# Left factors asked for sooner, and eighteen idle matmuls between the first transposes, in a two-layer decoder trunk

## The chip, the cores and the metric

One core of a Trainium2 chip (trn2) runs the kernel. The metric is the device time of one execution in microseconds (us); the time given is the median of several plain runs. A profiled execution is one run more, taken with the hardware profiler.

## The reference

The input is x of 512 positions by 1024 features, in float32. Two layers follow one another, each a mixer and a feed-forward, each with an RMS norm ahead and a residual add behind.

```python
for i in range(DEPTH):                       # DEPTH = 2
    hn = rmsnorm(h, mix_norm_g[i])
    if i % 2 == 0:
        h = h + sgu_mixer(hn, ...)           # gelu(hn @ w_in) -> u, v; LN(v) mixed over 128 positions; (u * mixed) @ w_out
    else:
        h = h + retention(hn, positions, ...)  # q, k rotated, decayed scores, v, gated by silu(g); @ w_out
    h = h + swiglu(rmsnorm(h, ffn_norm_g[i]), ...)   # (silu(a) * b) @ w_down, a and b 2816 wide
return rmsnorm(h, final_norm_g)
```

## The kernel before, in words

**Matrix products.** Every float32 product is made of three matmuls (`three`, L246): each factor is split into a high part in the fast fp32r format (`h`) and the rest (`l`), and h·h, h·l and l·h are summed in PSUM. For the weights ScalarE (ACT) writes `wh_...` (L216) and VectorE (DVE) writes `wl_...` = raw - `wh` (L223).

**Seven products instead of eight.** The large products (`seven`, L321) split both factors in quarters and use a Strassen-like scheme with the seven products P1, P7, P6, Q4, P5, P2, P3. For each of them the weight tile is a quarter or a sum of quarters. Such a sum is made in part by a DMA that adds while it writes: the first quarter is loaded through SyncE's queue (SP, L344), the next is added by a DMA that GpSimd (POOL) issues (L347). P6's weights come into being in P7's tile: once DVE has written P7's `wl`, POOL's DMA adds one more quarter to the raw tile, and ACT makes P6's `wh` from it. The raw tile's name in the program keeps the label P722 for all of P7, P6 and Q4.

**Left factors.** The other side, the activations, has sums as well. `combos` (L473) makes them for products whose left side is computed in the kernel, `xA` (L709) for the normed x of a feed-forward or of the retention. Each sum is a `Chain` of three steps: `total` (DVE, `xP7_...`, L737), `high` (ACT, `xP7h_...`, L740) and `low` (DVE, `xP7l_...`, L743). Asking for a sum (`ask=True`) runs the first step; each later job of the pipeline runs one more; a use without `ask` runs what is left. Asking sooner therefore moves these steps forward in the recorded order.

**The order.** `pipeline` (L92) records the jobs; a scheduler in the framework then orders the instructions of each engine by a timing model of its own. Every engine works off its own queue strictly in that order. A small move in the source can thus reorder several queues.

**The start.** x comes in four chunks of 128 positions. PE first runs five idle matmuls on a tile of ones (`wake`, L174 to L177), then transposes chunk 0 (`xT_in_0`, eight 128x128 transposes, L669), `mix_ps` (a small transpose of the gains, L193), and chunk 1 (`xT_in_1`) as soon as its load is there. ACT and DVE make the halves `XH_in` and `XL_in` of each chunk (L673, L674). The first projection (`ps_v0`, in two PSUM tiles for chunks 0 and 1 and for chunks 2 and 3) works chunk by chunk with four weight tiles of 512 KB, `wr_v0_0` to `wr_v0_3`, whose halves `wh_v0_i`, `wl_v0_i` are scaled by `mix_cols` (L219, L226).

**The end of the first mixer.** `into_x("so", ...)` multiplies by `sgu_w_out` and adds to `X`. Its last product P3 (PSUM tile `X_so`, left factor `y_P3h`, `y_P3l`) is made for two chunks, 12 matmuls each. After each, DVE adds to `X` (L530), ACT squares (`sq_so`), small DVE instructions make the norm's factor (`nf_so`), DVE scales (`xs_f0_c`, L687), PE transposes (`xT_f0_c`), and ACT and DVE make `XH_f0` and `XL_f0` of chunk c. Chunks 3 and 2 are done before P3, chunks 0 and 1 behind it.

**The first feed-forward's opening.** `project_t("gl0", ...)` (PSUM `ps_gl0`, weights `wh_gl0_k`) first runs on chunks 2 and 3, then P1 of unit 0 (`X_gu0_0`, 48 matmuls), also on chunks 2 and 3; then the rest of `gl0` on chunks 0 and 1; then P7 (`Y_gu0_0`), which needs `xP7h_f0` and `xP7l_f0`. The second layer's feed-forward (`..._f1`, `gl1`, `gu1`) is built in the same way.

## Time and profile before

| | before |
|---|---|
| median of 3 plain runs | 1204.01 us (1203.71 to 1204.62) |
| the profiled execution | 1207.73 us |
| its span, first to last instruction | 1206.0 us |
| PE (TensorE) busy | 1186.8 us, 98% |
| DVE (VectorE) busy | 924.9 us, 77% |
| ACT (ScalarE) busy | 644.4 us, 53% |
| POOL (GpSimd) busy | 160.8 us, 13% |
| mean granted TensorE clock | 0.996 |

A row of a timeline gives the start and the length in us, the engine, the source line, the operation and its tiles (without buffer numbers), the shapes, the count of merged instructions, and in brackets the idle time ahead of it with what ended it. `[3.09 <-DMA X<-in_x]` reads: idle for 3.09 us until the load of X landed. The window rows give, for each engine, busy us and count, and at the end the mean granted clock of TensorE, the mean busy share of the DMA engines, and GB/s. The rows of the chain of waits have start, length and what ran. Matmuls overlap: the recorded length of one is more than the distance to the next.

### The profile page before, as it was taken

How to read it: one execution, taken by the hardware profiler on the slowest of the kernel's cores; microseconds unless marked ns; L12 is line 12 of the kernel's file. 1: busy time of each engine (PE TensorE's matmuls, PEld its weight loads, DVE VectorE, ACT ScalarE, POOL GpSimd, SP SyncE). 2: the span in 40 equal slices, each digit the busy share in tenths (PEclk: the TensorE clock that was granted, in tenths of full speed). 3: DMA queues.
4: the chain of work that ended last, by engine and by line, in shares of the span. 5: the costliest groups of instructions: out<-in, count | busy, mean ns of one | idle time of the engine just before them, and what ended most of it. 6: DMA issues, size and time to landing. Idle time of an engine off the chain costs nothing.

```text
span 1206.0 us, 18055 instructions
## 1 busy us (share of the span) xinstructions
PE 1186.8 (98%) x7206; PEld 1064.2 (88%) x7206; DVE 924.9 (77%) x1095; ACT 644.4 (53%) x815; POOL 160.8 (13%) x143
## 2 busy tenths in 40 slices
PE   8999999999999999999999999999999999999997
PEld 6888799998999987888888888888899989999986
DVE  5587968698987698788674757879768697666897
ACT  5523657455444547655453645566555554454565
POOL 1000121121110130211101001130121021101210
PEclk9999999999999999999999999999999999999999
DMA  9912958777876787766566457878867788676892
GB/s 312 282 48 57 243 118 204 184 165 213 210 196 153 198 170 255 192 140 176 113 190 143 119 133 171 204 131 283 215 125 174 191 222 203 165 195 187 156 245 96
DMA packets 118981, 216.42 MB, mean 179 GB/s; under 512 B 7497, under 2 KB 20849, under 8 KB 118897
## 3 DMA queue, kind: packets, MB, share of 16 engines
q1 hardware_dynamic: 83888, 148.13, 36.7%
q0 software_dynamic: 34720, 66.61, 33.1%
q8 instruction: 56, 0.92, 0.3%
q10 hardware_dynamic: 288, 0.52, 0.1%
q14 instruction: 29, 0.23, 0.1%
HBM read 212.10 MB, written 2.10 MB: 178 GB/s over the span
## 4 chain that ended last, share of the span: by engine, by line
PE 88%; DMA 4%; issue 3%; DVE 2%; ACT 2%; POOL 1%; SPq 0%; DVEq 0%; POOLq 0%; ACTq 0%
PE X_gu L249 6%; PE X_gu L248 6%; PE X_gu L247 6%; PE Y_gu L248 3%; PE Y_gu L249 3%; PE Y_gu L247 3%; PE X_dn L247 3%; PE X_dn L248 3%; PE X_dn L249 3%; PE X_vg L247 2%; PE X_vg L248 2%; PE X_vg L249 2%; PE ps_qk L247 2%; PE ps_qk L248 2%; PE ps_qk L249 2%
## 5 line engine op out<-in xcount | busy, mean ns | idle before, releaser
L223 DVE TENSOR_TENSOR wl_gu_P<-wr_gu_P,wh_gu_P 128x1024 fp32r<-128x1024 f32 x120 | 144.6, 1219 | 43.9 <-ACT wh_gu_P L216 43.8
L216 ACT ACTIVATE wh_gu_P<-wr_gu_P 128x1024 fp32r<-128x1024 f32 x120 | 122.4, 1051 | 64.4 <-DVE wr_gu_P L375 37.6
L347 POOL DMA_DIRECT2D wr_gu_P<-in_ffn_w_gu x48 | 58.4, 1244 | 384.8 <-DMA wr_gu_P<-in_ffn_w_gu 176.6
L216 ACT ACTIVATE wh_dn_P<-wr_dn_P 128x1024 fp32r<-128x1024 f32 x72 | 69.2, 980 | 50.2 <-DVE wr_dn_P L375 12.9
L223 DVE TENSOR_TENSOR wl_vg_P<-wr_vg_P,wh_vg_P 128x1024 fp32r<-128x1024 f32 x48 | 58.3, 1220 | 34.3 <-ACT wh_vg_P L216 28.0
L223 DVE TENSOR_TENSOR wl_dn_P<-wr_dn_P,wh_dn_P 128x1024 fp32r<-128x1024 f32 x72 | 79.4, 1128 | 2.5 <-issue 2.2
L347 POOL DMA_DIRECT2D wr_vg_P<-in_ret_w_in x26 | 31.5, 1250 | 262.9 <-DMA wr_vg_P<-in_ret_w_in 89.6
L347 POOL DMA_DIRECT2D wr_dn_P<-in_ffn_w_down x36 | 42.0, 1239 | 179.7 <-DMA wr_dn_P<-in_ffn_w_down 89.2
L216 ACT ACTIVATE wh_vg_P<-wr_vg_P 128x1024 fp32r<-128x1024 f32 x48 | 49.6, 1055 | 27.9 <-DMA wr_vg_P<-in_ret_w_in 13.0
L248 PE MATMUL ps_qk<-XL_r,wh_qk 128*128 128x512 f32 (+1 forms) x160 | 55.6, 348 | 0.0
L247 PE MATMUL ps_qk<-XH_r,wh_qk 128*128 128x512 f32 (+1 forms) x160 | 55.3, 348 | 0.0
L249 PE MATMUL ps_qk<-XH_r,wl_qk 128*128 128x512 f32 (+1 forms) x160 | 55.1, 348 | 0.0
L248 PE MATMUL Y_gu<-xP7l_f,wh_gu_P 128*128 128x256 f32 x160 | 45.4, 284 | 0.9 <-DVE xP7l_f L743 0.9
L247 PE MATMUL Y_gu<-xP7h_f,wh_gu_P 128*128 128x256 f32 x160 | 45.4, 284 | 0.8 <-ACT xP7h_f L740 0.8
L247 PE MATMUL Z_gu<-XH_f,wh_gu_P 128*128 128x256 f32 x160 | 45.4, 284 | 0.0
L249 PE MATMUL X_gu<-XH_f,wl_gu_P 128*128 128x256 f32 x160 | 45.3, 283 | 0.0
L247 PE MATMUL X_gu<-XH_f,wh_gu_P 128*128 128x256 f32 x160 | 45.3, 283 | 0.0
L248 PE MATMUL X_gu<-xP6l_f,wh_gu_P 128*128 128x256 f32 x160 | 45.3, 283 | 0.0
L249 PE MATMUL X_gu<-xP6h_f,wl_gu_P 128*128 128x256 f32 x160 | 45.3, 283 | 0.0
L247 PE MATMUL X_gu<-xP5h_f,wh_gu_P 128*128 128x256 f32 x160 | 45.3, 283 | 0.0
L248 PE MATMUL X_gu<-xP5l_f,wh_gu_P 128*128 128x256 f32 x160 | 45.3, 283 | 0.0
L249 PE MATMUL X_gu<-xP5h_f,wl_gu_P 128*128 128x256 f32 x160 | 45.3, 283 | 0.0
(590 smaller groups left out, 4209.8 us busy)
## 6 DMA issues: line engine op xcount, KB each, us to landing
wr_gu_P<-in_ffn_w_gu SPq DMA_DIRECT2D x100, 512.0 KB, 5.0
wr_dn_P<-in_ffn_w_down SPq DMA_DIRECT2D x50, 512.0 KB, 5.4
wr_gu_P<-in_ffn_w_gu POOLq DMA_DIRECT2D x48, 512.0 KB, 7.7
wr_vg_P<-in_ret_w_in SPq DMA_DIRECT2D x40, 512.0 KB, 4.9
wr_dn_P<-in_ffn_w_down POOLq DMA_DIRECT2D x30, 512.0 KB, 7.0
wr_vg_P<-in_ret_w_in POOLq DMA_DIRECT2D x26, 512.0 KB, 6.7
wr_ro_P<-in_ret_w_out SPq DMA_DIRECT2D x20, 512.0 KB, 5.8
wr_qk<-in_ret_w_in SPq DMA_DIRECT2D x32, 256.0 KB, 3.1
```

The source lines that it names most:

```text
L216: nc.scalar.activation(h, s, AF.Copy)
L223: nc.vector.tensor_tensor(l, s, f32(h), ALU.subtract)
L247: nc.tensor.matmul(o, ah, bh, start=start, stop=False, skip_group_check=True)
L248: nc.tensor.matmul(o, ah, bl, start=False, stop=False, skip_group_check=True)
L249: return nc.tensor.matmul(o, al, bh, start=False, stop=stop, skip_group_check=True)
L347: nc.gpsimd.dma_start(raw[p, 0, g, s][:, 0:nk, :], source(b, g, s, nk), accum_op=ALU.add)
```

## The change

The five wake matmuls become a helper, `keep_awake(n, after)`, which chains its matmuls behind a given instruction. It is called once more, with 18 matmuls behind the last transpose of chunk 0. In `so` the left factor of P3 is asked for after the second half of Q4. In both feed-forwards the left factor of P7 is asked for after the second half of P1 in unit 0, ahead of the rest of `gl`, and P5, P6 and P3 one place sooner each, after the first, second and third quarter of that rest.

```diff
+WAKE2 = 18
...
-    wake = PS("wake")
-    for _ in range(WAKE):
-        nc.tensor.matmul(wake[:, 0, 0:P], ones, ones, start=True, stop=True)
-    done(wake)
+    def keep_awake(n, after=None):
+
+        wake = PS("wake")
+        for _ in range(n):
+            with tc.issue_after(after.ins) if after else nullcontext():
+                after = nc.tensor.matmul(wake[:, 0, 0:P], ones, ones, start=True, stop=True)
+        done(wake)
+
+    keep_awake(WAKE)
...
-            nc.tensor.transpose(ps[:, k, :], src[:, k * P:(k + 1) * P], ident)
+            xn["turned"] = nc.tensor.transpose(ps[:, k, :], src[:, k * P:(k + 1) * P], ident)
...
     done(turn(0, X[:, 0, :], "in"))
+    keep_awake(WAKE2, xn["turned"])
...
-    into_x("so", sgu_w_out[0], rows(0, KD), yA, normed("f0", ffn_g[0:1], raw_copy("f0")))
+    into_x("so", sgu_w_out[0], rows(0, KD), yA, normed("f0", ffn_g[0:1], raw_copy("f0")),
+           {("Q4", 1): lambda: yA("P3", 0, ask=True)})
...
-                  mid={("h", 0): lambda: xparts("P7", ask=True), ("h", 1): lambda: xparts("P5", ask=True), ("h", 2): lambda: xparts("P6", ask=True),
-                       ("h", 3): lambda: xparts("P3", ask=True)})
-        unit(0, between=rest)
+                  mid={("h", 0): lambda: xparts("P5", ask=True), ("h", 1): lambda: xparts("P6", ask=True),
+                       ("h", 2): lambda: xparts("P3", ask=True)})
+        unit(0, {("P1", 1): lambda: xparts("P7", ask=True)}, between=rest)
```

The queues move at three places.

PE at the start, before: the transposes of chunk 0, the gains, and then the chunks and the first products (`wh_v0_0` is the first weight tile, `wh_v0_1` the second; `ps_v0_0` holds chunks 0 and 1, `ps_v0_1` chunks 2 and 3).

```order
L669 MATMUL xT_in_0_108<-ident_76,X_95 128x128 x8
L193 MATMUL mix0_ps_104<-ident_76,mix0_rows_97 128x8
L669 MATMUL xT_in_1_139<-ident_76,X_95 128x128 x8
L247 MATMUL ps_v0_0_121<-wh_v0_0_125,XH_in_117 128x512
L669 MATMUL xT_in_2_180<-ident_76,X_95 128x128 x8
L248 MATMUL ps_v0_0_121<-wl_v0_0_126,XH_in_117 128x512
L249 MATMUL ps_v0_0_121<-wh_v0_0_125,XL_in_118 128x512
L247 MATMUL ps_v0_0_121<-wh_v0_0_125,XH_in_117 128x512
L247 MATMUL ps_v0_1_122<-wh_v0_0_125,XH_in_117 128x512
L248 MATMUL ps_v0_1_122<-wl_v0_0_126,XH_in_117 128x512
...
L669 MATMUL xT_in_3_233<-ident_76,X_95 128x128 x8
L247 MATMUL ps_v0_0_121<-wh_v0_1_154,XH_in_117 128x512
```

The same place in the changed kernel:

```order
L676 MATMUL xT_in_0_108<-ident_76,X_95 128x128 x8
L181 MATMUL wake_121<-ones_81 128x128 x5
L200 MATMUL mix0_ps_104<-ident_76,mix0_rows_97 128x8
L181 MATMUL wake_121<-ones_81 128x128 x13
L676 MATMUL xT_in_1_158<-ident_76,X_95 128x128 x8
L254 MATMUL ps_v0_0_140<-wh_v0_0_144,XH_in_117 128x512
L676 MATMUL xT_in_2_199<-ident_76,X_95 128x128 x6
...
L256 MATMUL ps_v0_0_140<-wh_v0_0_144,XL_in_118 128x512
L254 MATMUL ps_v0_0_140<-wh_v0_1_173,XH_in_117 128x512
L676 MATMUL xT_in_3_252<-ident_76,X_95 128x128 x8
```

The eighteen wakes stand between the chunks, with `mix0_ps` behind the fifth. The first use of `wh_v0_1` moves ahead of the transposes of chunk 3, and the two `ps_v0_1` matmuls with `wh_v0_0` and `wl_v0_0` move behind it. At the end of `so` on PE all 12 matmuls of the first half of P3 now stand ahead of the transposes of chunks 3 and 2, where before two of them did, and the 12 of the second half directly behind these, ahead of `ps_gl0`; on DVE `y_P3l` moves from behind `wl_gl0_0` to ahead of the two `X<-X,X_so` that follow Q4.

ACT in the first feed-forward, before: the halves of chunks 0 and 1 and the high parts of unit 0's weights (`wr_gu0_0_P722...` is the raw tile of P7 and P6, `s1` the copy of P1's result, `xr` copies of the transposed x for the sums).

```order
L673 ACTIVATE XH_f0_1270<-xT_f0_0_1453 128x8x128
L216 ACTIVATE wh_gu0_0_P1_0_2_1388<-wr_gu0_0_P111_0_2_1320 128x1024
L216 ACTIVATE wh_gu0_0_P7_0_0_1419<-wr_gu0_0_P722_0_0_1245 128x1024
L216 ACTIVATE wh_gu0_0_P7_0_2_1448<-wr_gu0_0_P722_0_2_1284 128x1024
...
L673 ACTIVATE XH_f0_1270<-xT_f0_1_1563 128x8x128
L216 ACTIVATE wh_gu0_0_P6_0_0_1494<-wr_gu0_0_P722_0_0_1245 128x1024
L706 ACTIVATE xr_f0_0_0_1464<-xT_f0_1_1563 128x4x128
```

And now:

```order
L223 ACTIVATE wh_gu0_0_P1_0_2_1407<-wr_gu0_0_P111_0_2_1339 128x1024
L223 ACTIVATE wh_gu0_0_P7_0_0_1438<-wr_gu0_0_P722_0_0_1265 128x1024
L680 ACTIVATE XH_f0_1289<-xT_f0_0_1472 128x8x128
...
L223 ACTIVATE wh_gu0_0_P6_0_0_1513<-wr_gu0_0_P722_0_0_1265 128x1024
L680 ACTIVATE XH_f0_1289<-xT_f0_1_1582 128x8x128
L223 ACTIVATE wh_gu0_0_P6_0_2_1546<-wr_gu0_0_P722_0_2_1303 128x1024
```

`XH_f0` of chunk 1 has moved behind P6's first `wh`, and on DVE its `XL_f0` behind P6's first `wl`. On PE `xT_f0_1` now stands behind 43 of the 48 matmuls of P1 instead of 30, directly ahead of the rest of `gl0` but for five. On POOL the first add into P6's tile now stands ahead of the add for P5's.

DVE in the second feed-forward, at P7's left factor, before:

```order
L223 TENSOR_TENSOR wl_gu1_0_P6_0_2_8155<-wr_gu1_0_P722_0_2_7929,wh_gu1_0_P6_0_2_8154 128x1024
L223 TENSOR_TENSOR wl_gu1_0_P2_0_0_8187<-wr_gu1_0_P221_0_0_8124,wh_gu1_0_P2_0_0_8186 128x1024
L737 TENSOR_TENSOR xP7_f1_8260<-xr_f1_1_0_7859,xr_f1_0_0_8091 128x1024
L737 TENSOR_TENSOR xP5_f1_8289<-xr_f1_0_0_8091,xr_f1_0_1_8092 128x1024
L743 SCALAR_TENSOR_TENSOR xP7l_f1_8259<-xP7_f1_8260,xP7h_f1_8258 128x1024
```

And now:

```order
L230 TENSOR_TENSOR wl_gu1_0_P6_0_2_8174<-wr_gu1_0_P722_0_2_7948,wh_gu1_0_P6_0_2_8173 128x1024
L744 TENSOR_TENSOR xP7_f1_8250<-xr_f1_1_0_7878,xr_f1_0_0_8110 128x1024
L230 TENSOR_TENSOR wl_gu1_0_P2_0_0_8206<-wr_gu1_0_P221_0_0_8143,wh_gu1_0_P2_0_0_8205 128x1024
L744 TENSOR_TENSOR xP5_f1_8284<-xr_f1_0_0_8110,xr_f1_0_1_8111 128x1024
L750 SCALAR_TENSOR_TENSOR xP7l_f1_8249<-xP7_f1_8250,xP7h_f1_8248 128x1024
```

Only the sum `xP7` has moved up, by one instruction; `xP7l` keeps its place behind P2's first `wl` and P5's sum.

## The prediction

> **What bounds the kernel now.** I read the page first, then the list of waits of TensorE (PE; releaser, total us, count, longest), then the timeline of each engine at the waits that the change touches.

> ```profile
> PE 1186.8 (98%) x7206; PEld 1064.2 (88%) x7206; DVE 924.9 (77%) x1095; ACT 644.4 (53%) x815; POOL 160.8 (13%) x143
> ```

> ```profile
> PE Y_gu L248 <- DVE xP7l_f L743: 0.9, 1, 0.9
> PE Y_gu L247 <- ACT xP7h_f L740: 0.8, 1, 0.8
> ```

> PE is busy for 98% of the span, so only its idle time and its clock can be won. The change touches three places where it waits: the start, the end of `so` (both below), and P7 in the second feed-forward (these two rows). Sums are made against the profiled execution: 1207.73 us, span 1206.0. It is 3.7 us above the 1204.01 median of the plain runs; I carry the difference over to the median.

> **Start.** PE's timeline; two windows (the last three numbers are granted clock, DMA share, GB/s); the chain of waits, for prices at full clock; ACT; and how long the first weight tiles took to land:

> ```profile
> 5.45 0.27 PE L193 MATMUL mix_ps<-ident,mix_rows 8*128 8x8 f32 x1
> 8.82 1.70 PE L669 MATMUL xT_in<-ident,X 128*128 128x128 f32 x8 [3.09 <-DMA X<-in_x]
> ...
> 15.59 0.47 PE L247 MATMUL ps_v<-wh_v,XH_in 128*128 128x512 f32 x1
> ```

> ```profile
> 0.00:10.00 10.00, 5.70 (x26) 4.94 (x27) 3.46 (x7) 3.84 (x5) 3.13 (x12) 0.96 0.75 238
> 10.00:20.00 10.00, 9.60 (x46) 7.68 (x45) 7.06 (x11) 8.22 (x13) 0.00 (x0) 0.87 1.05 362
> ```

> ```profile
> 14.96 0.87 PE xT_in L669 x8
> 15.83 0.23 PE ps_v L247
> ...
> 84.84 1.78 PE mix L976 x16
> ```

> ```profile
> 13.83 1.34 ACT L219 ACTIVATE wh_v<-wr_v,mix_cols 128x512 fp32r<-128x512 f32 x2
> ```

> ```profile
> DMA to landing us min/median/max: 5.6/5.8/7.2
> ```

> After 3.09 us of idling, PE runs at half clock for 3.4 us: 8% of the first window and 26% of the second, so from 9.2 to 12.6. The eighteen matmuls fill that gap. `mix` has their shape: two records per matmul, so 1.78 / 16 x 2 = 0.22 us each. 18 x 0.22 = 4.0 us from 5.45 on, with 0.27 for `mix_ps` between them, ends at 9.7. The next transposes then start 0.9 us later than now, but at full clock take 0.87 us instead of 1.70: they end at 10.6, as now.

> What follows does not gain, because of the new order on PE. The first matmul with the second weight tile (`wh_v0_1`) now stands ahead of the last chunk's transposes and of two `ps_v0_1` matmuls. PE reaches it after eight transposes (0.87) and six matmuls of 0.23, at about 12.9. That tile's load is issued by SP at 8.0 us and takes 5.8, so it lands at 13.8; ACT started on it at 13.83. Its first half takes ACT 0.7, so PE resumes at 14.5. Before, the same matmul ran at 15.59, but with those eight transposes and two matmuls (0.87 + 2 x 0.23 = 1.3 us) already done. So the start comes out at 14.5 + 1.3 - 15.6 = **+0.2 us**. Bounds: the shortest landing, 5.6, gives 0; a half-clock stretch set off by the new wait of 1.6 us would add up to 1.5. If a plain run of before had no slow stretch there, it would reach that point at the same 14.5 with the 1.3 us done: then the start costs 1.3 with no new stretch at all. `mix_cols`, now behind five wakes (1.1 us) and behind `XL_in` on DVE, is hidden: it holds up `wh_v0_0` by some 0.7 us, to 8.8 for its first half, and PE asks for that at 10.6.

> **End of `so`.** PE; the clock in two windows; DVE:

> ```profile
> 144.52 0.39 PE L247 MATMUL X_so<-wh_so_P,y_P3h 128*128 128x512 f32 x1
> ...
> 147.28 1.06 PE L669 MATMUL xT_f<-ident,xs_f 128*128 128x128 f32 x8 [1.27 <-DVE xs_f L687]
> 149.46 0.58 PE L247 MATMUL ps_gl<-XH_f,wh_gl 128*128 128x256 f32 x1 [1.11 <-ACT XH_f L673]
> ...
> 153.38 0.28 PE L247 MATMUL ps_gl<-XH_f,wh_gl 128*128 128x256 f32 x1
> ```

> ```profile
> 145.58:149.00 3.42, 1.50 (x12) 1.05 (x10) 3.42 (x4) 2.86 (x6) 0.44 (x1) 1.00 1.03 210
> 149.00:152.40 3.40, 2.94 (x7) 2.37 (x8) 3.40 (x4) 2.23 (x4) 0.50 (x1) 0.51 1.00 206
> ```

> ```profile
> 139.51 1.28 DVE L530 TENSOR_TENSOR X<-X,X_so 128x512 f32<-128x512 f32 x2 [1.44 <-PE X_so L249]
> ...
> 160.28 0.69 DVE L530 TENSOR_TENSOR X<-X,X_so 128x512 f32<-128x512 f32 x1 [1.19 <-PE X_so L249]
> ```

> From 144.52 to 153.38 PE does 12 X_so matmuls (0.23 each), 16 transposes (0.87 for eight) and one ps_gl: 4.6 us of work in 8.9. The 4.3 lost are the two waits, the half clock of 149.0 to 152.4 behind them, and drains. In the new order `y_P3l` (1.2 us) runs on DVE just ahead of the row at 139.51, in that row's 1.44 us of idle, and costs nothing there. PE then does 12 X_so (to 147.3), both transposes (147.28 is when the later `xs_f` was there), 12 more X_so, and at 151.7 finds XH_f and XL_f done. So PE is **4.3 us ahead**.

> **What takes that back: the first feed-forward.** PE, DVE, POOL and ACT:

> ```profile
> 175.40 0.39 PE L248 MATMUL ps_gl<-XL_f,wh_gl 128*128 128x256 f32 x1
> ...
> 186.78 0.28 PE L247 MATMUL Y_gu<-xP7h_f,wh_gu_P 128*128 128x256 f32 x1
> 186.90 0.28 PE L248 MATMUL Y_gu<-xP7l_f,wh_gu_P 128*128 128x256 f32 x1
> ```

> ```profile
> 163.72 1.28 DVE L687 SCALAR_TENSOR_TENSOR xs_f<-X,nf_so,g_f 128x1024 f32<-128x1024 f32 x1
> ...
> 167.18 3.48 DVE L223 TENSOR_TENSOR wl_gu_P<-wr_gu_P,wh_gu_P 128x1024 fp32r<-128x1024 f32 x3
> ```

> ```profile
> 169.94 2.47 POOL L347 DMA_DIRECT2D wr_gu_P<-in_ffn_w_gu  x2 [16.84 <-DVE wl_gu_P L223]
> ```

> ```profile
> 175.58 1.06 ACT L216 ACTIVATE wh_gu_P<-wr_gu_P 128x1024 fp32r<-128x1024 f32 x1 [1.49 <-DMA wr_gu_P<-in_ffn_w_gu]
> ```

> In the new order `xT_f` of chunk 1 has 5 instead of 18 X_gu matmuls behind it, and on ACT its `XH_f` stands behind `wh` of P6, which waits for a DMA that adds into the tile. PE: 151.7 + 96 ps_gl (0.12 each, as from 186.78 to 186.90) + 0.87 = 164.1; 43 X_gu, so xT_f from 169.3 to 170.1; five more, and at 170.7 it needs XH_f, two matmuls on XL_f. DVE: the second `X<-X,X_so` comes at 153.1, behind two XL_f and a `wl_gl`. Before, `xs_f` of chunk 1 followed it by 3.44 us (160.28 to 163.72); now two `wl_gl` and `xs_f` of chunk 0 stand between, 3.5 us: 160.0 to 161.2. Three `wl_gu` of 1.13: 164.6. POOL's add follows 0.4 later and lands after 5.64 us (169.94 to 175.58): 170.6. Then `wh` takes 1.0, XH_f is done at 172.6, and XL_f, behind `wl` of P6, at 174.1. PE idles for about 2.0 + 1.1 us and passes at 174.1 instead of 175.40: **1.3 of the 4.3 us remain**. Bounds: if the add is early, XH_f follows xT_f at once, XL_f is ready at 172.4, and 3.0 remain; an add 1 us later leaves 0.3. P7's turn comes 11.4 us later (175.40 to 186.78), at 185.5; by the same chain `xP7l` is ready at 183.2 to 184.7 (three adds now share the DMA engines ahead of it), so nothing is lost there.

> Will the new idling halve the clock? At `so` 1.9 us of idle in 3.42 did, with transposes as the rest; 0.8 us in the second feed-forward did not. Here matmuls stand around the idle; I assume no stretch. [...]

> **Second feed-forward.** DVE, then PE:

> ```profile
> 891.65 2.36 DVE L223 TENSOR_TENSOR wl_gu_P<-wr_gu_P,wh_gu_P 128x1024 fp32r<-128x1024 f32 x2 [2.96 <-ACT wh_gu_P L216]
> 893.93 2.35 DVE L737 TENSOR_TENSOR xP_f<-xr_f,xr_f 128x1024 f32<-128x1024 f32 x2
> 896.33 1.23 DVE L743 SCALAR_TENSOR_TENSOR xP7l_f<-xP_f,xP7h_f 128x1024 fp32r<-128x1024 f32 x1
> ```

> ```profile
> 897.61 0.38 PE L248 MATMUL Y_gu<-xP7l_f,wh_gu_P 128*128 128x256 f32 x1 [0.88 <-DVE xP7l_f L743]
> ```

> P7's sum moves ahead of the second `wl_gu` (1.13 us), so `xP7h` comes 0.8 us sooner. But `xP7l` still stands behind that `wl_gu` and P5's sum in DVE's queue: 892.8 + 3 x 1.14 = 896.2 instead of 896.33. PE's first wait goes, its second grows by as much: **-0.1 us**. The bound is all of both waits, -1.7.

> **Sum.** +0.2 - 1.3 - 0.1 = -1.2: 1204.01 - 1.2 = 1202.8 us.

> **The rivals.** (1) *The lead at `so` survives*: the add lands early and PE stays 3.0 us ahead, or P7's waits go too. 0.2 - 3.0 - 0.1 = -2.9: 1201.1; with P7's 1.7 gone, 1199.5. For it speaks that the add waits only for DVE's `wl_gu`, which would come 3.5 us sooner if nothing stood between; against it, that three more DVE instructions and the order of ACT's queue do stand there. (2) *Slower, by the clock*: the new wait at 170.7 to 174.1 sets off a half-clock stretch (3.4 us, 1.5 us of work lost), and the plain runs of before do not hold the profile's two stretches (they are 3.7 us faster than the profile), so that what is saved on them is nil: 1.5 at `so` (half of 3.4 us, less the idle up to 149.46), 1.1 at the start. -1.2 + 1.5 + 2.6 = +2.9: 1206.9. It decides at an idle share of a window somewhere between 25% (0.8 us, no drop) and 56%. (3) *Waits merely traded*: only the new stretch, -1.2 + 1.5 = +0.3: 1204.3. The change then does what it says and moves nothing.

> **How the numbers follow.** 0.2%, 2.4 us, is about what a measurement can tell. Forecast 0.40, (3) 0.22, (1) 0.20, (2) 0.18. Forecast and (3) lie within 2.4 us; (1) is nearly all faster, (2) nearly all slower: 0.21 faster, 0.60 no change, 0.19 slower. The range reaches just beyond (1)'s first price and to that of (2): 1200.8 to 1206.9.

> **What would show it.** Right: no slow clock at 9 us, a PE wait of 1.6 us for `wh_v` near 13; no wait for `xs_f` at 147; a PE wait of 2 to 3 us for XH_f and XL_f at 171 to 174, with `wh_gu_P` on ACT released by a DMA just ahead; P7's wait near 895 whole, but on `xP7l` alone. Wrong: PE passes from X_gu to ps_gl without a wait, or the clock row shows a new half.

## The result and the profile after

| | before | after |
|---|---|---|
| median of 22 runs each | 1204.08 us (1202.20 to 1207.19) | 1206.29 us (1204.21 to 1209.95) |
| the profiled execution | 1207.73 us | 1205.57 us |
| its span | 1206.0 us | 1203.5 us |

The ratio after to before is 1.0016, with a 95% interval of 1.0009 to 1.0023: the change costs about 2 us here. (A second set of runs, e5 below, has it at +1.2.) The forecast was 1.2 us faster. The two profiled executions say the opposite of the runs, 2.2 us faster, since that of before lies above its median by 3.7 us and that of after below its own by 0.7. So these two traces show where waits went, and what they cost has to come from the runs.

The page of after, PE's busy time; it holds the 36 records of the eighteen new matmuls:

```profile
PE 1189.1 (99%) x7242; PEld 1067.5 (89%) x7242; DVE 924.3 (77%) x1095; ACT 643.9 (53%) x815; POOL 160.8 (13%) x143
```

PE's waits in after, the longest first (total us, count, longest). Gone are the wait for X at the start and the one for `xs_f` at the end of `so`; two for `XH_f` and `XL_f` are new and among the longest:

```profile
PE ps_gl L254 <- ACT XH_f L680: 1.9, 1, 1.9
PE wake L181 <- POOL eps L171: 1.2, 1, 1.2
PE ps_gl L255 <- DVE XL_f L681: 1.0, 1, 1.0
```

PE's timeline in after, at the places of the prediction: the start, P3 of `so`, the rest of `gl0`, and P7 in both layers.

```profile
5.50 1.68 PE L181 MATMUL wake<-ones 128*128 128x128 f32 x10
...
7.27 3.17 PE L181 MATMUL wake<-ones 128*128 128x128 f32 x26
10.28 1.04 PE L676 MATMUL xT_in<-ident,X 128*128 128x128 f32 x8
...
13.66 0.50 PE L254 MATMUL ps_v<-wh_v,XH_in 128*128 128x512 f32 x1
...
143.96 0.39 PE L254 MATMUL X_so<-wh_so_P,y_P3h 128*128 128x512 f32 x1
...
146.69 1.91 PE L676 MATMUL xT_f<-ident,xs_f 128*128 128x128 f32 x16
...
168.85 1.04 PE L676 MATMUL xT_f<-ident,xs_f 128*128 128x128 f32 x8
...
172.34 0.50 PE L254 MATMUL ps_gl<-XH_f,wh_gl 128*128 128x256 f32 x2 [1.87 <-ACT XH_f L680]
173.82 0.58 PE L255 MATMUL ps_gl<-XL_f,wh_gl 128*128 128x256 f32 x1 [0.98 <-DVE XL_f L681]
...
186.58 0.28 PE L254 MATMUL Y_gu<-xP7h_f,wh_gu_P 128*128 128x256 f32 x1
...
895.22 0.39 PE L255 MATMUL Y_gu<-xP7l_f,wh_gu_P 128*128 128x256 f32 x1 [0.22 <-DVE xP7l_f L750]
```

`so` runs through without a wait, as forecast. But at `Y_gu` of the first layer PE is 0.2 us ahead of the profile of before (186.58 against 186.78), where the forecast left 1.1 (1.3 at `so`, less 0.2 from the start). ACT shows who holds up `XH_f` of chunk 1: `wh` of P6, released by the DMA that adds.

```profile
170.32 1.06 ACT L223 ACTIVATE wh_gu_P<-wr_gu_P 128x1024 fp32r<-128x1024 f32 x1 [4.77 <-DMA wr_gu_P<-in_ffn_w_gu]
171.28 1.01 ACT L680 ACTIVATE XH_f<-xT_f 128x1024 fp32r<-128x1024 f32 x1
```

The granted clock was half from 9.13 to 12.55 and from 149.08 to 152.49 us in the trace of before, and from 173.59 to 177.00 in that of after; in both also at the very end, from 1203.80 and 1201.00 on. Rows of before, then of after (PE busy us is the first number after the length, the granted clock the third from the end):

```profile
9.13:12.55 3.42, 3.42 (x17) 3.06 (x16) 2.53 (x4) 1.02 (x1) 0.00 (x0) 0.50 1.02 360
12.55:149.08 136.53, 134.12 (x633) 110.82 (x632) 99.02 (x171) 65.82 (x98) 13.67 (x11) 1.00 0.62 181
149.08:152.49 3.41, 3.03 (x8) 2.45 (x9) 3.41 (x4) 2.24 (x4) 0.59 (x1) 0.50 0.97 199
152.49:1203.80 1051.31, 1041.37 (x6532) 943.58 (x6530) 817.34 (x915) 571.52 (x709) 143.41 (x120) 1.00 0.71 178
```

```profile
177.00:1201.00 1024.00, 1016.22 (x6341) 919.62 (x6340) 800.37 (x887) 559.24 (x690) 139.13 (x116) 1.00 0.72 180
1201.00:1203.50 2.50, 0.00 (x0) 0.00 (x0) 0.00 (x0) 0.00 (x0) 0.00 (x0) 0.50 0.40 148
```

```profile
170.17:173.59 3.42, 0.80 (x5) 0.39 (x3) 2.19 (x2) 1.97 (x2) 0.55 (x1) 1.00 1.11 201
173.59:177.00 3.41, 3.18 (x15) 3.18 (x16) 0.17 (x1) 0.25 (x1) 0.66 (x1) 0.50 0.77 116
177.00:180.41 3.41, 3.41 (x30) 3.41 (x30) 1.45 (x2) 3.41 (x5) 0.93 (x2) 1.00 0.38 69
```

The window with 0.80 us of work is followed by one at half clock, which the forecast had assumed away.

### The profile page after: what moved, and what is told of

It is laid out like the page before. It is cut to its first block, busy times and chain, and to the rows that moved or that the text cites. A ratio compares the mean times of both kernels' runs of the same rounds, so it can differ in the third digit from the quotient of the medians.

```text
span 1203.5 us, 18132 instructions
## 1 busy us (share of the span) xinstructions
PE 1189.1 (99%) x7242; PEld 1067.5 (89%) x7242; DVE 924.3 (77%) x1095; ACT 643.9 (53%) x815; POOL 160.8 (13%) x143
## 5 line engine op out<-in xcount | busy, mean ns | idle before, releaser
L223 ACT ACTIVATE wh_gu_P<-wr_gu_P 128x1024 fp32r<-128x1024 f32 x120 | 122.5, 1052 | 64.3 <-DVE wr_gu_P L382 35.7
L223 ACT ACTIVATE wh_dn_P<-wr_dn_P 128x1024 fp32r<-128x1024 f32 x72 | 69.3, 981 | 50.9 <-DVE wr_dn_P L382 12.5
L223 ACT ACTIVATE wh_vg_P<-wr_vg_P 128x1024 fp32r<-128x1024 f32 x48 | 49.5, 1054 | 27.6 <-DMA wr_vg_P<-in_ret_w_in 11.4
L255 PE MATMUL X_gu<-XL_f,wh_gu_P 128*128 128x256 f32 x160 | 45.4, 283 | 0.0
L254 PE MATMUL X_gu<-xP6h_f,wh_gu_P 128*128 128x256 f32 x160 | 45.3, 283 | 0.0
L255 PE MATMUL Z_gu<-XL_f,wh_gu_P 128*128 128x256 f32 x160 | 45.3, 283 | 0.0
L256 PE MATMUL Z_gu<-XH_f,wl_gu_P 128*128 128x256 f32 x160 | 45.3, 283 | 0.0
```

The costliest lines, as they stand in the source:

```text
L223: nc.scalar.activation(h, s, AF.Copy)
L254: nc.tensor.matmul(o, ah, bh, start=start, stop=False, skip_group_check=True)
L255: nc.tensor.matmul(o, ah, bl, start=False, stop=False, skip_group_check=True)
L256: return nc.tensor.matmul(o, al, bh, start=False, stop=stop, skip_group_check=True)
```

## The experiments

Theory T: the loss is made near 172 us, where the early request in `so` puts `XH_f` and `XL_f` of chunk 1 behind P6's halves, and PE's waits for them set off a half clock. Rival R: it is made at the start, by the eighteen idle matmuls. All runs of one group share the runs of the kernel before. Where two new kernels are compared with one another, I use the means of their 11 or 12 runs, since the runs of one kernel spread over 2 to 6 us and a median of 11 moves in jumps; the standard error of such a difference is 0.3 to 0.7 us.

### The parts alone

e1, the kernel before with only this:

```diff
+    keep_awake(WAKE2, xn["turned"])
```

> The kernel before with the eighteen idle matmuls alone. Theory T (the loss is made by the new wait at 170 to 174 us, which the early request in `so` brings): the start is worth nothing or little, 0 to -0.8 us against before; in its profile PE reaches the first X_so<-wh_so_P,y_P3h at 143.9 to 144.6, without a half clock near 9 us, and everything behind it is as before. Rival R (the loss is made at the start: in plain runs of before the clock is seldom halved there, and the matmuls only push the transposes back): +1.5 to +2.2 us here, nearly all of the change's loss. The profile of the changed kernel holds no half clock at the start either way; the median decides.

e2, the kernel before with only this:

```diff
+           {("Q4", 1): lambda: yA("P3", 0, ask=True)})
```

> The kernel before with the early request of P3's left factor in `so` alone. Theory T: +2 to +4 us against before. The 3 to 4 us of idle saved at the end of `so` are returned 20 us later as PE waits for XH_f and XL_f (1.5 to 2 and 1 us), and those waits halve the clock for 3.4 us (1.5 us more) in most runs, while the median run of before had lost less at `so` than its profile. Rival R: within 1 us of before, since what is lost at the start isn't here.

e3, the kernel before with only this (and P5, P6, P3 one place sooner in `rest`):

```diff
-        unit(0, between=rest)
+        unit(0, {("P1", 1): lambda: xparts("P7", ask=True)}, between=rest)
```

> The kernel before with the early request of P7's left factor in the two feed-forwards alone. Theory T: the second feed-forward gains -1.0 to -2.2 us (P7's two waits at 897 us fall from 1.7 to about 0.2), the first nothing, since the order of ACT at XH_f of chunk 1 is as in the kernel before. The forecast's own step said -0.1 here: then within 0.5 us of before.

e4, e1 and e3 together:

> The change without the early request in `so`. Theory T: -1 to -3 us against before, the sum of the two single parts, since nothing of the new wait near 172 us is here. Rival R: +1 to +2 us, the loss at the start with nothing to set against it. If the second feed-forward gains nothing in plain runs, T gives 0 to -0.8.

| | median, us | mean less mean of before (1204.98) | ratio, 95% interval |
|---|---|---|---|
| before, 35 runs | 1205.14 | | |
| e1 idle matmuls | 1204.12 | +0.1 | 1.0003, 0.9992 to 1.0014 |
| e2 request in `so` | 1204.93 | +0.2 | 1.0006, 0.9995 to 1.0016 |
| e3 requests in the feed-forwards | 1205.35 | +0.1 | 0.9999, 0.9991 to 1.0008 |
| e4 e1 and e3 | 1205.53 | +0.6 | 1.0003, 0.9994 to 1.0013 |

No part alone makes the 2 us, none gains, and every interval holds 1. T's +2 to +4 for e2 missed, its -1 to -2.2 for e3 as well, and R's +1.5 to +2.2 for e1 too. For e4 both missed: T had -1 to -3, or 0 to -0.8 if the second feed-forward gains nothing, and R +1 to +2. The order of ACT at `XH_f` of chunk 1 is that of the change in e2, and PE's waits are there, but the lead that `so` gave pays for them. e4's trace shows what that lead is against. In PE's timeline of e4, `so` is as in the kernel before, and in this execution the clock stayed whole:

```profile
144.41 0.39 PE L254 MATMUL X_so<-wh_so_P,y_P3h 128*128 128x512 f32 x1
...
147.17 1.06 PE L676 MATMUL xT_f<-ident,xs_f 128*128 128x128 f32 x8 [1.27 <-DVE xs_f L694]
149.35 0.39 PE L254 MATMUL ps_gl<-XH_f,wh_gl 128*128 128x256 f32 x1 [1.11 <-ACT XH_f L680]
...
151.87 0.28 PE L254 MATMUL ps_gl<-XH_f,wh_gl 128*128 128x256 f32 x1
```

From 144.41 to 151.87 are 7.5 us, where the profile of before took 8.9 (144.52 to 153.38) for the same rows. So 1.4 of the 4.3 us that I took for the gain at `so` are a half clock that not every execution has. Most of the traced ones do have it: e1 and e3, with the same order at `so`, show it as the profile of before does, so it is there in three of four. The grid window of those waits and the one behind it, in e1, then in e3:

```profile
145.76:149.17 3.41, 1.42 (x10) 1.21 (x11) 3.41 (x4) 2.92 (x6) 0.00 (x0) 1.00 1.07 249
149.17:152.59 3.42, 3.42 (x10) 2.67 (x9) 2.99 (x3) 2.66 (x5) 0.00 (x0) 0.50 0.97 199
```

```profile
145.51:148.92 3.41, 1.27 (x10) 0.85 (x8) 3.41 (x4) 3.08 (x6) 0.00 (x0) 1.00 1.03 226
148.92:152.34 3.42, 3.18 (x8) 2.60 (x9) 3.42 (x4) 2.25 (x5) 0.00 (x0) 0.50 1.07 243
```

The waits of e2 and of the next group's e6 (the change without idle matmuls) are alike, 1.16 + 0.98 and 1.11 + 0.98 us. How they lie in the windows of 3.41 us is not. Windows of e2, then of e6:

```profile
169.07:172.48 3.41, 1.27 (x9) 0.85 (x7) 2.36 (x2) 1.77 (x2) 0.88 (x1) 1.00 1.14 208
172.48:175.90 3.42, 3.42 (x17) 3.42 (x18) 0.00 (x0) 0.93 (x1) 0.32 (x1) 0.50 0.90 134
```

```profile
168.12:171.54 3.42, 2.31 (x20) 2.10 (x18) 1.23 (x2) 1.97 (x2) 0.00 (x0) 1.00 1.12 199
171.54:174.95 3.41, 2.43 (x20) 2.23 (x19) 1.13 (x1) 0.01 (x1) 1.20 (x1) 1.00 1.04 162
```

In e2 both waits fall into one window, which does 1.27 us of work, and half clock follows. In e6 they lie in two, with 2.31 and 2.43 us of work, and the clock stays whole. Where the grid lies in e6 is an estimate from its start: the eight transposes from 10.27 us on took 1.21 us to the next row, those at half clock 1.59 (8.11 to 9.70) and those at whole clock 0.79 (13.87 to 14.66), so the half clock there ended near 11.1 us, and 47 times 3.413 us later is 171.5.

### The change again, without its idle matmuls, and without the wait

e5 is the changed kernel once more. e6 is e5 without the `keep_awake(WAKE2, ...)` line. e7 is e5 with P6's halves in unit 0 of the first layer made three jobs later, which puts `XH_f` and `XL_f` of chunk 1 ahead of them on ACT and DVE:

```diff
-        behind = {"Q4": behind} if "P6" in onto else {}
+        behind = ({"P6": 3, "Q4": 1} if name == "gu0_0" else {"Q4": behind}) if "P6" in onto else {}
```

e8 is e7 without the `keep_awake(WAKE2, ...)` line.

> The changed kernel a second time, beside the kernel before on the same chip. The single parts came out within 0.2 us of before in the mean, the whole change 2.0 us slower on another chip. If the loss belongs to the change (theory T, the waits near 172 us and the half clock that they set off): +1 to +2.5 us against before, and a half clock directly behind the windows in which PE waits for XH_f and XL_f. If it was the draw of the runs or of the chip: within 0.6 us.

> The change without the eighteen idle matmuls. Theory T: as the whole change, +1 to +2.5 us against before, since the waits near 172 us are here. Rival R (the loss needs the idle matmuls at the start): within 0.6 us of before.

> The whole change, with the halves of P6's weights in unit 0 of the first feed-forward made three jobs later, so that XH_f and XL_f of chunk 1 stand ahead of them on ACT and DVE and wait for no DMA that adds. Theory T: PE's two waits near 172 us fall from 2.9 to 1 to 1.7 us in sum, too little in one window of 3.41 us for a half clock, and the lead of `so` survives: PE reaches Y_gu<-xP7h_f 2.5 to 4 us sooner than in the changed kernel; -1 to -2.5 us against before, -3 to -4 against the change. Rival R: the same as the change, +1 to +2.

> The same as the run ahead of it, without the eighteen idle matmuls. Theory T: within 0.6 us of that run, -1 to -2.5 us against before; if the idle matmuls cost something (R), another 1 to 2 us faster than that run; if they save something, slower by 0.5 to 1.

| | median, us | mean less mean of before (1205.36) | ratio, 95% interval |
|---|---|---|---|
| before, 33 runs | 1205.23 | | |
| e5 the change | 1206.42 | +1.2 | 1.0009, 0.9997 to 1.0020 |
| e6 without idle matmuls | 1204.79 | -0.3 | 1.0001, 0.9991 to 1.0010 |
| e7 P6 later | 1203.89 | -1.0 | 0.9994, 0.9984 to 1.0005 |
| e8 P6 later, without idle matmuls | 1203.21 | -2.4 | 0.9984, 0.9975 to 0.9993 |

Both theories hold half. Taking the wait away gains 2.3 us with the idle matmuls (e5 to e7) and 2.1 without (e6 to e8). Taking the idle matmuls away gains 1.6 (e5 to e6) and 1.4 (e7 to e8). T alone would have had e6 as slow as e5; R alone would have had e7 as slow as e5. The sizes were missed too: T had -3 to -4 for e7 against e5, and e7 by itself is not clear of before (its interval holds 1).

What the wait costs is read in PE's timeline, from the transposes of chunk 1 to the first matmul of P7; first and last row of e5, of e6 and of e7, in this order (e7 with its two waits):

```profile
170.58 1.04 PE L676 MATMUL xT_f<-ident,xs_f 128*128 128x128 f32 x8
...
189.45 0.28 PE L254 MATMUL Y_gu<-xP7h_f,wh_gu_P 128*128 128x256 f32 x1
```

```profile
168.50 1.03 PE L676 MATMUL xT_f<-ident,xs_f 128*128 128x128 f32 x8
...
184.09 0.28 PE L254 MATMUL Y_gu<-xP7h_f,wh_gu_P 128*128 128x256 f32 x1
```

```profile
170.38 1.03 PE L676 MATMUL xT_f<-ident,xs_f 128*128 128x128 f32 x8
172.53 0.50 PE L254 MATMUL ps_gl<-XH_f,wh_gl 128*128 128x256 f32 x2 [0.53 <-ACT XH_f L680]
173.79 0.38 PE L255 MATMUL ps_gl<-XL_f,wh_gl 128*128 128x256 f32 x1 [0.76 <-DVE XL_f L681]
...
185.16 0.28 PE L254 MATMUL Y_gu<-xP7h_f,wh_gu_P 128*128 128x256 f32 x1
```

The same work takes 14.8 us in e7, 15.6 in e6, 17.1 in e2 (168.11 to 185.24), 17.7 in the profile of the change (168.85 to 186.58) and 18.9 in e5. So the waits cost 0.8 us more than e7's without a half clock, and 2.3 to 4.1 with one. e5 has the longest, since there the half clock lasts two windows:

```profile
171.06:174.48 3.42, 1.55 (x13) 1.24 (x10) 1.33 (x2) 1.97 (x2) 0.00 (x0) 1.00 1.12 204
174.48:177.89 3.41, 2.43 (x12) 2.33 (x12) 1.03 (x1) 0.77 (x1) 1.20 (x1) 0.50 0.82 115
177.89:181.31 3.42, 3.42 (x18) 3.42 (x18) 1.98 (x2) 3.42 (x6) 1.47 (x2) 0.50 0.65 118
```

The first half window holds part of the wait, PE works for only 2.43 us of it, and the next one is half again.

What the request in `so` brings and loses is seen best over the whole way from the first matmul of P3 in `so` to the first of P7, 296 records of PE in every kernel here. The start falls out of this. The us of that way in each profiled execution:

| order | with a half clock on the way | with the whole clock |
|---|---|---|
| no request in `so`: before, e1, e3; e4 | 42.3, 42.4, 42.3 | 40.9 |
| request in `so`: the change, e2, e5; e6 | 42.6, 42.0, 43.8 | 40.5 |
| request in `so`, P6 later: e7 to e12 | none | 39.7 in each |

The request trades one chance of a half clock, at `so`, for another near 172 us. With P6 later neither came in six executions, which agree within 0.02 us.

In e7 the waits are 0.53 + 0.76 us. Its ACT shows `XH_f` started by its own transposes, with P6's `wh` behind it:

```profile
171.46 1.02 ACT L680 ACTIVATE XH_f<-xT_f 128x1024 fp32r<-128x1024 f32 x1 [3.44 <-PE xT_f L676]
...
174.74 2.01 ACT L223 ACTIVATE wh_gu_P<-wr_gu_P 128x1024 fp32r<-128x1024 f32 x2
```

The start in e5 and e8, PE's timeline of each, then ACT's of each. The row that starts at 15.34 in e5 and at 14.32 in e8 is the first matmul with `wh_v0_1`:

```profile
13.46 0.40 PE L256 MATMUL ps_v<-wh_v,XL_in 128*128 128x512 f32 x1
15.34 0.50 PE L254 MATMUL ps_v<-wh_v,XH_in 128*128 128x512 f32 x1 [1.48 <-ACT wh_v L226]
15.68 1.03 PE L676 MATMUL xT_in<-ident,X 128*128 128x128 f32 x8
```

```profile
7.74 1.94 PE L676 MATMUL xT_in<-ident,X 128*128 128x128 f32 x8 [1.99 <-DMA X<-in_x]
...
13.53 1.03 PE L676 MATMUL xT_in<-ident,X 128*128 128x128 f32 x8
14.32 0.48 PE L254 MATMUL ps_v<-wh_v,XH_in 128*128 128x512 f32 x1
```

```profile
14.57 1.34 ACT L226 ACTIVATE wh_v<-wr_v,mix_cols 128x512 fp32r<-128x512 f32 x2 [1.92 <-DMA wr_v<-in_sgu_w_in]
```

```profile
12.75 1.34 ACT L226 ACTIVATE wh_v<-wr_v,mix_cols 128x512 fp32r<-128x512 f32 x2 [0.30 <-DMA wr_v<-in_sgu_w_in]
```

With the idle matmuls PE stands before the second weight tile, with the last chunk's transposes still to do behind it. Without them it does these first; in e8 it comes to that matmul 0.9 us after the first half of `wh_v0_1` is done (12.75 and half of 1.34, against 14.32), so there PE's own work sets the time, with the transposes of chunk 1 at half clock (1.94 us, where those of the last chunk take 1.03) in it. The pair shows the order and not its price: the tile landed 1.8 us later in e5 (ACT starts on it at 14.57) than in e8 (12.75).

### Cover for the landing, and the two requests apart

e9 is e7 with the first projection recorded in another order, so that six more matmuls that need only the first weight tile stand ahead of the first one with `wh_v0_1` on PE:

```diff
-        for c in range(i):
-            natural_step(vps[c // 2][:, c % 2, :], c, i, v0w[i])
-        for kp in range(i + 1):
+        for kp in range(i):
             natural_step(vps[i // 2][:, i % 2, :], i, kp, v0w[kp])
+        for c in range(i + 1):
+            natural_step(vps[c // 2][:, c % 2, :], c, i, v0w[i])
```

e10 is e9 without the eighteen idle matmuls. e11 is e8 once more (on the chip of the first time after all), and e12 is e8 without the requests in the feed-forwards.

> The change with P6's halves three jobs later, and with six matmuls of the first projection that need only the first weight tile moved ahead of the first one that needs `wh_v0_1` (the eighteen idle matmuls stay). If the idle matmuls cost their 1 to 1.6 us because the new order on PE leaves nothing to do while the second weight tile lands (it landed at 12.8 to 14.6 us, PE waited 0.2 to 1.5 us), six matmuls of 0.23 us fill that wait: -0.7 to -1.4 us against the kernel without them, so -1.5 to -2.2 us against before, and PE's wait for `wh_v` near 14 us is gone or below 0.5. If they cost it because the transposes of chunk 1 run 2 to 3 us after their load has landed, nothing comes back: -0.5 to -1 against before.

> The same without the eighteen idle matmuls. Before, PE had 1.3 us of other work ahead of the first matmul with `wh_v0_1`, now 2.7. If the landing of that tile bounds the start, -0.3 to -1 us against the kernel with P6 later and no idle matmuls; if PE's own work bounds it, the same as that kernel within 0.4.

> The early requests in `so` and in both feed-forwards, with P6's halves three jobs later, without idle matmuls, on another chip: -1.4 to -2.4 us against before, as the first time (1203.21 beside 1205.23).

> The early request in `so` alone, with P6's halves three jobs later, without idle matmuls and without the early request in the feed-forwards. If that request is worth the 0.5 to 1.7 us by which PE's way through 862 to 917 us was shorter in the profiles that have it: slower than the run ahead of it by 0.5 to 1.2 us. If it is worth 0.1 as forecast, or nothing, as the single run of it had it: within 0.4 us of it.

| | median, us | mean less mean of before (1204.94) | ratio, 95% interval |
|---|---|---|---|
| before, 35 runs | 1204.62 | | |
| e9 P6 later, idle matmuls with cover | 1202.73 | -2.3 | 0.9980, 0.9971 to 0.9988 |
| e10 the same without idle matmuls | 1202.95 | -1.9 | 0.9985, 0.9976 to 0.9993 |
| e11 P6 later, without idle matmuls | 1203.09 | -2.0 | 0.9980, 0.9971 to 0.9988 |
| e12 e11 without the feed-forward requests | 1203.16 | -1.5 | 0.9987, 0.9978 to 0.9996 |

With cover the idle matmuls cost nothing that these runs can tell (e9 against e10, -0.4 in the means); e9 stands at -2.3 against before, where e7, without the cover, had -1.0. So it is the order that they bring, not the time that they take, that costs. PE and ACT in e9, at the same place as above; the second weight tile's first half is done while PE still has work, and no wait stands at 14.51. The tile landed early in this execution, and the change's own profile, where ACT starts on it at 12.89, has next to no wait either; that the cover counts rests on the runs.

```profile
14.29 0.39 PE L256 MATMUL ps_v<-wh_v,XL_in 128*128 128x512 f32 x1
14.51 0.40 PE L254 MATMUL ps_v<-wh_v,XH_in 128*128 128x512 f32 x1
```

```profile
12.78 1.34 ACT L226 ACTIVATE wh_v<-wr_v,mix_cols 128x512 fp32r<-128x512 f32 x2 [0.67 <-DMA wr_v<-in_sgu_w_in]
```

Without them the cover brings nothing (e10 against e11): there PE's own work was long enough. e11 repeats e8. e12 is 0.5 us from e11 in the means and 0.1 in the medians, which these runs do not tell from nothing. e8 to e12 all beat the kernel before, by 0.1 to 0.2% and with intervals below 1.

## Why the prediction was wrong, point by point

**"I assume no stretch" is the step that failed**, in the term for `so` and the first feed-forward. Up to there the mechanism was right: the measured waits were 1.87 and 0.98 us, forecast 2.0 and 1.1, and the add into P6's tile was the cause. What follows them was put at nothing, which no run shows for such waits in one window: the change, e2 and e5 have half clock behind them. The prediction's own row at `so` spoke against that: 1.9 us of idling in one window had a half clock behind it, and here 3.1 were forecast. The reason it gave, that matmuls and not transposes stand around the idle, did not hold. The change's two profiles and e2's have the half clock, e6's does not: there the waits, 2.09 us in all, lie in two windows by the estimate above. Against e7, between 0.8 and 4.1 us go there, and 2.1 to 2.3 in the mean of the runs (e7 and e8). Over the way from P3 to P7 the four profiles with the request and P6 in its place take 42.2 us on average, the four without the request 42.0: the lead of 4.3 us was taken back whole, not by 3.0, and the term of -1.3 came out at +0.2. The runs of e2, the request alone, say the same, +0.2.

**The sum was made against one execution, and carried over to the median.** At `so` this did less harm than it looks: with a whole clock the loss there is 2.9 us and not 4.3, but three of four executions have the half clock. What the profile of before holds beyond its median lies mostly elsewhere. From the first matmul of P7 in the first layer to its second one in the second layer (186.78 to 897.61) it takes 710.8 us, and the other thirteen profiles 708.2 to 709.0, so some 2 of the 3.7 us were lost there. The change's own profile, 2.2 us below that of before, has the sign that such a sum gives; the 22 runs of each do not.

**Start, +0.2.** The mechanism was right: PE asks for `wh_v0_1` with the work that used to cover it still to do. The forecast time, 14.5 us, is near the mean (13.54, 14.10, 13.66, 15.34 and 15.18 in the profiles of e1, e4, the change, e5 and e7, mean 14.4), but each follows the landing of the tile. Mis-sized was what it was compared with. In the profile of before the same matmul ran at 15.59; in the seven profiles without idle matmuls and without cover (before, e2, e3, e6, e8, e11, e12) it ran at 14.28 to 16.10, mean 15.0. With the 1.3 us of work still to do that makes +0.7. The four pairs of runs with and without the idle matmuls (e1 and before, e4 and e3, e5 and e6, e7 and e8) give +0.1, +0.4, +1.6 and +1.4 us in the means, 0.9 on average; the upper bound of the prediction, 1.3 to 1.5, holds it.

**Second feed-forward, -0.1.** Right within what can be told, but not by the rows that it was read from. In the pair of profiles P7's second matmul moved by 2.4 us (897.61 to 895.22), more than my bound of 1.7. Here too the profile of before is the odd one: it alone waits for `xP7h` (0.84 us) and then for `xP7l` (0.88). e1, e2 and e12, with the same order, wait for `xP7l` alone, 0.88, 0.77 and 0.40 us; the ten profiles with the request, 0.22 to 0.47. The way from P7 to P7 is no shorter for it, 708.7 us on average with the request and in these three without. The runs, +0.1 for e3 and -0.5 for e11 against e12, cannot tell -0.1 from nothing.

**The signs.** As named: no slow clock at 9 us, no wait for `xs_f`, and the wait for `XH_f` and `XL_f` with P6's `wh` just ahead on ACT. Not as named: P7's wait near 895 was 0.22 us and not whole, and the 1.6 us wait for `wh_v` is not in the change's profile, since the tile was there sooner (12.9 us, forecast 13.8) and PE later (the transposes behind the idle matmuls start at 10.3, forecast 9.7); e4, e5 and e7 have 1.06 to 1.48 of it. The new half clock was named as the sign of being wrong.

**The rivals.** Rival (2), half clock anew and the profile's savings nil, gave 1206.9 and comes nearest to 1206.29. Its new half clock is there. Its other half is not borne out: it had the plain runs of before without the profile's two stretches, but the one at the start is in all eight profiles without idle matmuls (the transposes of chunk 1 or of chunk 2 take 1.86 to 1.94 us in each, those of chunk 3 1.03 or 1.04), and the one at `so` in three of four. So its number is in part luck. The start does cost something near its 1.3 us, but because of the order on PE, not because the half clock was missing.

**What stays open.** Runs other than the profiled ones give a mean clock only. How many of the change's longer runs owe their time to the place near 172 us, and how many to the start or elsewhere, is inferred from e6 to e9 and not seen. The change was measured at +1.9 us in the means, and the second time at +1.2 with an interval that reaches 1; the terms as found, +0.2, +0.9 and -0.1, make +1.0, and whether the rest is more than scatter is not shown. The wait for `XH_f` is 1.87 us in the change and e5 and 1.11 to 1.16 in e2 and e6, and ACT's wait for the add into P6's tile 4.77 and 4.79 us in the first two, 4.09 and 4.02 in the others; why is open. Whether the feed-forward requests are worth 0.5 us or nothing was not settled.

## What to carry to other kernels

Before a sum is made against a trace, look in other executions which of its half-clock stretches and late landings come back, and leave out those that do not. Price a new wait with the half clock that waits of that size had behind them in the same trace. A lead won at one place is worth only what the next wait in line leaves of it; look who stands ahead of the needed instruction on its engine's queue, and move that first. Work put ahead to keep TensorE busy was free here only where the order behind it still covered the next load (-0.4 us from e10 to e9, against 1.4 and 1.6 from e8 to e7 and e6 to e5).

## What the runs showed of the hardware

The grid of 3.413 us was measured in the traces of before and after (the multiples of 40, 308 and 300 above). It lies elsewhere in each of six executions: counted from the first instruction, the line at which a half clock near 149 us or at 172 to 175 us begins is 0.40 (e5), 1.81 (e2), 2.15 (e3), 2.31 (before), 2.40 (e1) and 2.92 us (the change) past a whole multiple of 3.4133 (1024.00 / 300). Windows with 0.32 (before, 5.72 to 9.13 us), 0.80 (the change), 1.27 (e2, e3), 1.41 (before, 145.67 to 149.08), 1.42 (e1) and 1.55 us (e5) of PE work were followed by half clock; the row with 1.50 us quoted in the prediction is that of 1.41, taken 0.09 us sooner. Windows with 2.56 and 2.53 us of work in before (893.19 to 896.60 and on to 900.01) and 2.31 and 2.43 in e6 were not. Nor was one with 2.13 in e7 (171.32 to 174.73 us), but no change of its clock shows where the grid lies there. In both, the way from the wait for `XL_f` to P7 took the 11.4 us of whole clock (172.72 to 184.09 in e6, 173.79 to 185.16 in e7, 175.40 to 186.78 before). Out of half clock, a window with 2.43 us of work (e5) was followed by another half one, those with 3.03 (before, 149.08 to 152.49) and 3.18 (the change) by a whole one. So no single long gap was needed here: the window with 0.80 us of work had no wait longer than 1.87 us, and the one with 1.55 idled for little more than half its length. And nearly the same waits came with 1.5 us more or without, by the draw (17.1 us in e2, 15.6 in e6).

In e4 the clock stayed whole over transposes and waits. Two windows of 3.41 us at `so`, then the first one's transposes (`xT_f`) alone:

```profile
144.97:148.38 3.41, 2.00 (x17) 1.55 (x15) 3.41 (x4) 2.35 (x6) 0.41 (x1) 1.00 0.99 207
148.38:151.80 3.42, 2.45 (x11) 2.07 (x12) 3.42 (x4) 2.25 (x4) 0.00 (x0) 1.00 1.09 259
```

```profile
144.97:148.38 3.41, 2.00 (x16) 1.55 (x15) 0.00 (x0) 1.13 (x2) 1.00 0.99 207
```

All of its 2.00 us are transposes, and the clock was whole in it and in the one behind it. If these float32 transposes had not counted as work, this would have been a window without any, and elsewhere windows with 0.32 to 1.55 us of work were followed by half clock. So I take it that here they counted. It is an inference from one execution, and no change of the clock near these windows shows that they lie on e4's grid.
